# Another order of the seven Strassen products in an FFN up-projection, and a lower priority for the end of a norm

## Chip, cores and metric

The kernel runs on one core of one Trainium2 chip. The metric is the device time of one execution in microseconds (us), given as the median of the runs; lower is better.

## What is computed

One layer of a transformer with two half-step FFNs (macaron form) around a token mixer, on 1024 tokens of width 1024, d_ff 2816, all in fp32:

```python
def swiglu(h, w1, w3, w2):
    return (jax.nn.silu(h @ w1) * (h @ w3)) @ w2

def reference(x, ...):
    h = rmsnorm(x, ffn1_norm[l])
    x = x + 0.5 * swiglu(h, ffn1_w1[l], ffn1_w3[l], ffn1_w2[l])
    h = rmsnorm(x, mix_norm[l])
    x = x + token_mix(h, ...)          # differential attention and sparse attention
    h = rmsnorm(x, ffn2_norm[l])
    x = x + 0.5 * swiglu(h, ffn2_w1[l], ffn2_w3[l], ffn2_w2[l])
    return rmsnorm(x, final_norm)
```

The change lies in h @ w1 and h @ w3 of both FFNs and in the RMS norm behind FFN1.

## The kernel before

**Tiling.** Activations lie transposed, 128 features on the partitions and 512 tokens (TB) in a row; the 1024 tokens are two such halves, tb 0 and 1. Every fp32 product is made of three matmuls: operands are split into a high part (whi, hi) and a low rest (wlo, lo), and high x high, high x low and low x high are added up in PSUM. A weight is split by ScalarE (line 86, the high part) and VectorE (line 82, the low part: source minus high part). A matmul's stationary operand is 128 x 128 of a weight, its moving one 128 x 512 of the activations.

**FFN up-projection (ffn_up).** The 22 blocks f of 128 columns of w1 and w3 are taken in 11 pairs fp. The first two pairs (NPLAIN) are plain products. The other nine, per FFN, use the Winograd form of Strassen's algorithm on 2 x 2 blocks: the two f of a pair by the two halves of the 1024 features, against the two feature halves by the two token halves. It has seven products in place of eight. Each product has two results m (0 for w1, 1 for w3), and each m takes 4 blocks x 3 = 12 matmuls, so a product is 24 and a pair 168. The moving operands (B11, B21, B22 and T[0] to T[3]) are made once per FFN (right_sums). The weights are, by their names in the code: A11, A12 and A22 as loaded, and the sums S1 = A21 + A22, S3 = A11 - A21, S2 = S1 - A11, S4 = A12 - S2 (lines 352 to 355, on GpSimd, for the first pair on VectorE). S3 is written over a21 and S2 over a11, so a11 must be split before S2 is formed.

The products accumulate in three pairs of PSUM banks, X, Y and Z, each with m = 0 and 1, one buffer each:

| bank | products in their order | what reads the bank, and where |
|---|---|---|
| X | A11 B11, then A12 B21 on top | after A11: ScalarE copies it to s1 (line 343); after A12: Silu on ScalarE (348) and a multiply on VectorE (349) give c11 |
| Y | S2 T1, then S3 T2, then A22 T3 on top | after each: VectorE adds s1 into u2, u3 and c21 (363) |
| Z | S1 T0, then S4 B22 on top | after each: VectorE adds into u3 and u2 (370) |

A bank that is read in the middle of its sum must have been read before the next matmul accumulates into it. finish_a applies the Silu and the multiply (408, on GpSimd) and stores the result; act_sums forms four differences of a pair's results on GpSimd (378) and stores them in DRAM (379; saT in the trace), for the down-projection's own Strassen form. These run in place on u2, c21 and u3, whose tiles have one buffer. s1 has one buffer too.

**Weights around it.** a11 and a12 are loaded into two buffers (wst), a21, a22, s1 and s4 into one each, all by SP's DMA queue (line 332). Split weights have four slots (two pools of two). Between the products 13 jobs per FFN are handed out: left_sums loads two blocks of w2, forms four sums on VectorE (400) and stores them (402); plain_sums does the activations' differences for the two plain pairs, with four loads (386) into four tiles of their own.

**The end of FFN1 (ffn_down, after1).** The last of the seven down products updates x for the first half of the features of tb 1. For each block, after1 stores x, splits it for the next stage and adds its square to nacc (line 152). After the eighth, norm_final makes a matmul with a matrix of ones (tot, line 163) to sum over partitions, and the reciprocal root R from it (165, and 117 to 122), at a high priority (HOT = 400). The mixer's first products (gm, lines 49 to 51 under raw_unit) use the split x without R; their results are multiplied by R after the product. They have four banks.

**What sets the order.** The program is written with tiles and without semaphores. A planner at build time simulates the program and gives each engine a fixed queue: among the instructions whose inputs and buffers it takes to be ready it picks the one first in program order, shifted by a priority. At run time the queues run in order and wait for one another where data demand it. So TensorE's order need not be the program's, and the planner may cut a product in pieces.

Of the kernel before, what the change touches and what calls it, by code (L numbers as in the profile page):

```python
# [15 lines left out]
P = 128  # L16
T = 1024
# [137 lines left out]
        norm_final(K, tb)  # L155


def norm_final(K, tb):
    nc = K.nc
    del K.seen[tb]  # L160
    with K.tc.high_priority(offset=HOT):
        tot = K.pt.tile([P, TB], F32, tag="acc", name="tot")
        nc.tensor.matmul(tot, lhsT=K.ones, rhs=K.acc[tb], start=True, stop=True)  # L163
        m = K.np.tile([P, TB], F32, tag=f"nsq{tb * K.sq2}", name="nm")
        nc.vector.tensor_scalar(out=m, in0=tot, scalar1=1.0 / D, scalar2=EPS, op0=ALU.mult, op1=ALU.add)
        K.R[tb] = K.rp.tile([P, TB], F32, tag=f"R{tb}", name="R")
        K.rdone = newton_rsqrt(nc, K.R[tb], K.acc[tb], m, nc.vector)
# [97 lines left out]
def ffn_up(K, w13, w2, ctxt, ctx0, gi, first):  # L265
# [7 lines left out]
    def form(src):  # L273
        hi, lo = split_fresh(K, K.nw, src)
        K.nw += 1
        return hi, lo
# [34 lines left out]
    with ctx:  # L311
        rw = open_pool(K, ctx, "up_raw", 1)
        po = open_pool(K, ctx, "up_post", 1)
        ex = open_pool(K, ctx, "up_ex", 1)
        jobs = [lambda j=j: left_sums(K, ex, w2, j) for j in range(NF // 2)]
        jobs[4:4] = [lambda p=p: plain_sums(K, ex, p) for p in range(NPLAIN)]
        raw = lambda n: rw.tile([P, KD, P], F32, tag=n, name=n)
        B11, B21, B22 = K.h[0][0:h], K.h[0][h:], K.h[1][h:]

        def prod(o, w, m, x, start):  # L320
            for k in range(h):
                for i, (a, b) in enumerate(((0, 0), (0, 1), (1, 0))):
                    K.mark = nc.tensor.matmul(o, lhsT=w[a][:, m * h + k], rhs=x[k][b], start=start and k == 0 and i == 0,  # L323
                                              stop=k == h - 1 and i == 2, skip_group_check=True)

        for fp in range(NPLAIN, NF // 2):
            f0, f1 = 2 * fp, 2 * fp + 1
            a11 = K.wst.tile([P, KD, P], F32, tag="wst", name="a11")
            a12 = K.wst.tile([P, KD, P], F32, tag="wst", name="a12")
            a21, a22, s1, s4 = raw("a21"), raw("a22"), raw("s1"), raw("s4")  # L330
            for t, f, j in ((a11, f0, 0), (a21, f1, 0), (a22, f1, 1), (a12, f0, 1)):
                nc.sync.dma_start(out=t, in_=w13[f, j])
            u = {}
            for n in ("s1", "u2", "u3", "c21", "c11"):
                for m in range(2):
                    if n != "c11" or m == 0:
                        u[n, m] = po.tile([P, TB], F32, tag=f"{n}{m}", name=n)
            X, Y, Z = [[bank(n, m) for m in range(2)] for n in "XYZ"]

            w = form(a11)  # L340
            for m in range(2):
                prod(X[m], w, m, B11, True)
                nc.scalar.activation(out=u["s1", m], in_=X[m], func=AF.Copy)
            w = form(a12)
            for m in range(2):
                prod(X[m], w, m, B21, False)
            c = u["c11", 0]
            nc.scalar.activation(out=c, in_=X[0], func=AF.Silu)
            nc.vector.tensor_tensor(out=c, in0=X[1], in1=c, op=ALU.mult)
            store(f0, 0, c)  # L350
            se = nc.vector if fp == NPLAIN else nc.gpsimd
            se.tensor_tensor(out=s1, in0=a21, in1=a22, op=ALU.add)
            se.tensor_tensor(out=a21, in0=a11, in1=a21, op=ALU.subtract)
            se.tensor_tensor(out=a11, in0=s1, in1=a11, op=ALU.subtract)
            se.tensor_tensor(out=s4, in0=a12, in1=a11, op=ALU.subtract)
            done = (fp - NPLAIN) * len(jobs) // (NF // 2 - NPLAIN), (fp + 1 - NPLAIN) * len(jobs) // (NF // 2 - NPLAIN)
            for job in jobs[done[0]:done[1]]:
                job()
            for src, x, n in ((a11, T[1], "u2"), (a21, T[2], "u3"), (a22, T[3], "c21")):
                w = form(src)  # L360
                for m in range(2):
                    prod(Y[m], w, m, x, n == "u2")
                    nc.vector.tensor_tensor(out=u[n, m], in0=Y[m], in1=u["s1", m], op=ALU.add)  # L363
                if n == "c21":
                    finish_a(K, u[n, 0], u[n, 1], f1, 0, store)
            for src, x, n, f in ((s1, T[0], "u3", f1), (s4, B22, "u2", f0)):
                w = form(src)
                for m in range(2):
                    prod(Z[m], w, m, x, n == "u3")
                    nc.vector.tensor_tensor(out=u[n, m], in0=Z[m], in1=u[n, m], op=ALU.add)  # L370
                finish_a(K, u[n, 0], u[n, 1], f, 1, store if n == "u3" else lambda *_: None)
            act_sums(K, u["c11", 0], u["u2", 0], u["c21", 0], u["u3", 0], u["c21", 1], u["u2", 1], u["u3", 1], fp)


def act_sums(K, b11, b12, b21, b22, t1, t2, t4, j):
# [5 lines left out]

def plain_sums(K, ex, j):
    t = {}
    for n in ("B11", "B12", "B21", "B22"):
        t[n] = ex.tile([P, TB], F32, tag=n, name="pa")
        K.nc.sync.dma_start(out=t[n], in_=K.s_a[n][j])
    act_sums(K, t["B11"], t["B12"], t["B21"], t["B22"], t["B11"], t["B22"], t["B21"], j)


# [930 lines left out]
def body(tc, A, out):  # L1320
# [5 lines left out]
    with ExitStack() as ctx:  # L1326
# [27 lines left out]
        with ExitStack() as c0, ExitStack() as c1:  # L1354
            K.wpools = [K.whl, open_pool(K, c0, "whl2", B_W, side="right")]
            xp = open_pool(K, c1, "x", 1)
            K.np, K.sq2 = open_pool(K, c1, "norm1", 2), 1
            K.pt = open_pool(K, c1, "tot1", 2, True)
            K.x = x_tiles(xp, "x")
            log_exp(K)  # L1360
            first = []
            for tb in range(NTB):
                for k in range(KD):
                    if tb == 0 and k % 2 == 0:
                        first.append(load_fresh(K, k // 2, A["f1w13"][k // 4, k // 2 % 2]))
                    nc.sync.dma_start(out=K.x[tb][k], in_=A["x"][tb, :, k])
                    if tb == 0:
                        norm_split(K, 0, k, 0)
                    norm_stat(K, tb, k, nc.gpsimd if tb and k in (1, 3, 5) else nc.vector)
            K.sq2 = 0  # L1370

            def after1(tb, d):
                nc.sync.dma_start(out=K.s_x[tb][d], in_=K.x[tb][d])
                norm_split(K, tb, d, 1)
                norm_stat(K, tb, d, nc.vector, tb == 0)
            ffn(K, A["f1w13"], A["f1w2"], c1, 0, first, lambda tb, k: A["x"][tb, :, k], after1)
        mix(K)
        with ExitStack() as c2:
# [120 lines left out]
```

## Time and profile before

| | us |
|---|---|
| median of 3 runs | 3003.48 (2998.64 to 3005.93) |
| profiled execution, its own time | 3003.5 |
| its span, first to last instruction | 3001.7 |
| TensorE busy | 2872.7 (96%) |
| VectorE, ScalarE, GpSimd busy | 1956.4, 1274.2, 979.9 |
| FFN1: the nine Strassen pairs of the up-projection | 100.9 to 465.1 |
| FFN2: the same | 2409.0 to 2771.9 |

Engines are named as the profile does: PE is TensorE's matmul, PEld its weight load, DVE VectorE, ACT ScalarE, POOL GpSimd, SP the engine whose queue issues the DMAs (SPq). L323 is line 323. "Y<-tf,whi" is an instruction that writes tile Y from tiles tf and whi. PEclk is the granted TensorE clock as a share of 2.4 GHz. Time in brackets before an instruction is idle time of its engine, with what ended it. Times of a timeline are from the start of the span.

### The profile page before, as it was taken

The numbers are of one execution on the slowest core, as the hardware profiler recorded it, in microseconds if no ns is written. First come the engines' busy times: TensorE is split into PE (matmuls) and PEld (weight loads), VectorE is DVE, ScalarE is ACT, GpSimd is POOL, SyncE is SP. The second block draws the span as 40 slices with busy tenths as digits, with TensorE's granted clock in tenths as the row PEclk, the third lists the DMA queues.
The fourth block names the chain that finished last, engine by engine and source line by source line (L and its number), as shares of the span: only waits on it lengthen the run. The fifth ranks groups of instructions, "written<-read, shape, count | busy, mean of one in ns | idle before, by whom it ended". The sixth has DMA issues, their size and how long they took to land. (4 is left out here: it accounts for less than half of the span.)

```text
span 3001.7 us, 39937 instructions
## 1 busy us (share of the span) xinstructions
PE 2872.7 (96%) x14238; PEld 2395.9 (80%) x14238; DVE 1956.4 (65%) x3140; ACT 1274.2 (42%) x2195; POOL 979.9 (33%) x765
## 2 busy tenths in 40 slices
PE   9999999999999999799899999999999999999998
PEld 7777777887888778678788888888877877777886
DVE  8665666665687567676677777776433866566656
ACT  6322224442333245345566666666433422222443
POOL 4555551000044223222232333333232456553101
PEclk9999999999999999899999999999999999999999
DMA  4443448655456544544332234222842155445854
GB/s 140 173 162 133 174 163 303 200 191 150 148 184 241 192 159 148 185 160 164 130 109 85 85 115 160 77 83 73 301 141 100 62 204 171 141 164 181 288 183 147
DMA packets 212710, 478.19 MB, mean 159 GB/s; under 512 B 20896, under 2 KB 39584, under 8 KB 212512
## 3 DMA queue, kind: packets, MB, share of 16 engines
q1 hardware_dynamic: 212512, 475.65, 46.1%
q8 instruction: 112, 1.84, 0.3%
q14 instruction: 86, 0.70, 0.1%
HBM read 313.56 MB, written 162.00 MB: 158 GB/s over the span
## 5 line engine op out<-in xcount | busy, mean ns | idle before, releaser
L49 PE MATMUL gm<-hi,whi 128*128 128x512 f32 x880 | 353.4, 402 | 5.5 <-ACT whi L86 1.8
L51 PE MATMUL gm<-hi,wlo 128*128 128x512 f32 x880 | 350.2, 399 | 0.0
L50 PE MATMUL gm<-lo,whi 128*128 128x512 f32 x880 | 350.0, 398 | 0.0
L747 PE MATMUL S<-kt,qt 128*128 128x320 f32 (+5 forms) x1152 | 274.6, 352 | 45.7 <-ACT Pt L756 16.1
L82 DVE TENSOR_TENSOR tl<-tr,th 128x512 fp32r<-128x512 f32 (+2 forms) x384 | 236.3, 619 | 82.2 <-ACT th L86 78.5
L86 ACT ACTIVATE th<-tr 128x512 fp32r<-128x512 f32 (+2 forms) x384 | 204.1, 543 | 201.5 <-PE tr L797 197.2
L323 PE MATMUL Y<-tf,whi 128*128 128x512 f32 x864 | 275.0, 397 | 9.8 <-DVE u L363 9.8
L82 DVE TENSOR_TENSOR wlo<-st,whi 128x1024 fp32r<-128x1024 f32 x154 | 198.2, 1304 | 119.6 <-ACT whi L86 119.0
L754 DVE CUSTOM_DVE_ANT_0 S<-S,slab 128x896 f32<-128x896 f32 (+7 forms) x320 | 224.6, 709 | 71.5 <-PE S L747 67.1
L49 PE MATMUL acc<-whi 128*128 128x512 f32 (+1 forms) x628 | 243.4, 388 | 3.3 <-DVE u L370 3.3
L50 PE MATMUL acc<-wlo,whi 128*128 128x512 f32 (+1 forms) x628 | 243.4, 388 | 0.0
L51 PE MATMUL acc<-whi,wlo 128*128 128x512 f32 (+1 forms) x628 | 243.1, 389 | 0.0
L86 ACT ACTIVATE whi<-st 128x1024 fp32r<-128x1024 f32 x154 | 160.5, 1057 | 186.9 <-PE acc L51 124.6
L904 POOL TENSOR_SCALAR Ps<-Ps,l 128x384 f32<-128x384 f32 (+7 forms) x128 | 101.3, 791 | 421.8 <-DVE l L902 201.6
L747 PEld LDWEIGHTS S<-kt,qt 128*128 128x128 f32 x1152 | 183.6, 190 | 69.1 <-ACT Pt L756 17.2
L82 DVE TENSOR_TENSOR wlo<-a,whi 128x1024 fp32r<-128x1024 f32 x90 | 159.8, 1779 | 83.1 <-ACT whi L86 79.8
L323 PEld LDWEIGHTS Y<-tf,whi 128*128 128x128 f32 x864 | 162.6, 189 | 51.4 <-DVE u L363 14.7
L49 PEld LDWEIGHTS gm<-hi,whi 128*128 128x128 f32 x880 | 169.5, 193 | 39.9 <-issue 4.1
L51 PEld LDWEIGHTS gm<-hi,wlo 128*128 128x128 f32 x880 | 169.2, 192 | 36.8 <-DVE wlo L82 0.6
L50 PEld LDWEIGHTS gm<-lo,whi 128*128 128x128 f32 x880 | 169.2, 192 | 31.3
L323 PE MATMUL Y<-tf,wlo 128*128 128x512 f32 x432 | 171.0, 397 | 2.8 <-DVE wlo L82 2.8
L950 PE MATMUL o<-th,vt 128*128 128x256 f32 (+1 forms) x608 | 164.5, 287 | 1.8 <-ACT th L86 1.7
(313 smaller groups left out, 6968.6 us busy)
## 6 DMA issues: line engine op xcount, KB each, us to landing
wst<-in_win_dram SPq DMA_DIRECT2D x55, 512.0 KB
sw<-w2s SPq DMA_DIRECT2D x44, 512.0 KB
st<-sw SPq DMA_DIRECT2D x88, 256.0 KB
st<-saT SPq DMA_DIRECT2D x88, 256.0 KB
a<-in_f1w_dram SPq DMA_DIRECT2D x36, 512.0 KB
a<-in_f2w_dram SPq DMA_DIRECT2D x36, 512.0 KB
st<-saB SPq DMA_DIRECT2D x66, 256.0 KB
qt<-sq SPq DMA_DIRECT2D x128, 128.0 KB
```

What stands on the lines that cost most here:

```text
L49: first = nc.tensor.matmul(out, lhsT=w[0][:, wk], rhs=x[0], start=start, stop=False, skip_group_check=skip)
L50: nc.tensor.matmul(out, lhsT=w[0][:, wk], rhs=x[1], start=False, stop=False, skip_group_check=skip)
L51: nc.tensor.matmul(out, lhsT=w[1][:, wk], rhs=x[0], start=False, stop=stop, skip_group_check=skip)
L82: return nc.vector.tensor_tensor(out=lo, in0=src, in1=hi.bitcast(F32), op=ALU.subtract)
L86: nc.scalar.activation(out=hi, in_=src, func=AF.Copy)
L323: K.mark = nc.tensor.matmul(o, lhsT=w[a][:, m * h + k], rhs=x[k][b], start=start and k == 0 and i == 0, stop=k == h - 1 and i == 2, skip_g ...
L747: K.last = nc.tensor.matmul(S[:, o:o + n], lhsT=q, rhs=k[:, k0 + c:k0 + c + n], start=i == 0, stop=i == 1)
L754: nc.vector.tensor_tensor_reduce(out=sv, in0=sv, in1=mv, scale=-0.125, scalar=BIG, op0=ALU.add, op1=ALU.min, accum_out=nm)
L904: nc.gpsimd.tensor_scalar(out=p[:, 0:n], in0=p[:, 0:n], scalar1=l[:, c:c + 1], scalar2=1.0, op0=ALU.mult, op1=ALU.mult)
L950: nc.tensor.matmul(dst, lhsT=v, rhs=hi[:, b * P:(b + n) * P], start=False, stop=False, skip_group_check=True)
```

## The change

In ffn_up the order in the program becomes, per pair: S2 into Y, S1 into Z, A12 into X, S3 into Y, then the loads of the next pair and its A11 into X, then A22 into Y and S4 into Z. The A11 product of the first pair stands ahead of the loop. The tile s1 (now s0 and s1 of a new pool) gets two buffers. The adds of one product stand behind both of its m, apart from those of S4. The first weight splits of a pair are asked for in the order S2, S1, A12, S3, and A22 and S4 after the next A11. The jobs stay behind the A12 product. plain_sums takes its four tiles out of the two buffers that left_sums uses.

For FFN1's second token half the end of the norm (norm_final) is called by after1 with a priority of -60, so it stands behind instructions that follow it by about that many places, and not 400 places ahead.

```diff
-def norm_final(K, tb):
+def norm_final(K, tb, hot=HOT):
...
-    with K.tc.high_priority(offset=HOT):
+    with K.tc.high_priority(offset=hot):
...
+        po2 = open_pool(K, ctx, "up_s1", 2)
...
+        def load(fp):
...
+            r = [a11, a12] + [raw(n) for n in ("a21", "a22", "s1", "s4")]
+            for t, f, j in ((a11, f0, 0), (r[2], f1, 0), (r[3], f1, 1), (a12, f0, 1)):
                 nc.sync.dma_start(out=t, in_=w13[f, j])
+            return r
+
+        def first_product(r):
+            X = [bank("X", m) for m in range(2)]
+            w = form(r[0])
+            s = []
+            for m in range(2):
+                prod(X[m], w, m, B11, True)
+                s.append(po2.tile([P, TB], F32, tag=f"s{m}", name="s1"))
+                nc.scalar.activation(out=s[m], in_=X[m], func=AF.Copy)
+            return X, s
+
+        n0, n1 = NPLAIN, NF // 2
+        r = load(n0)
+        X, sv = first_product(r)
+        for fp in range(n0, n1):
...
+            se.tensor_tensor(out=s1, in0=a21, in1=a22, op=ALU.add)
+            se.tensor_tensor(out=a21, in0=a11, in1=a21, op=ALU.subtract)
+            se.tensor_tensor(out=a11, in0=s1, in1=a11, op=ALU.subtract)
+            se.tensor_tensor(out=s4, in0=a12, in1=a11, op=ALU.subtract)
+            ws2, ws1, wa12, ws3 = form(a11), form(s1), form(a12), form(a21)
+
+            def add(n, o, i):
+                for m in range(2):
+                    nc.vector.tensor_tensor(out=u[n, m], in0=o[m], in1=i[m], op=ALU.add)
             for m in range(2):
-                prod(X[m], w, m, B11, True)
-                nc.scalar.activation(out=u["s1", m], in_=X[m], func=AF.Copy)
-            w = form(a12)
+                prod(Y[m], ws2, m, T[1], True)
+            add("u2", Y, sv)
             for m in range(2):
-                prod(X[m], w, m, B21, False)
+                prod(Z[m], ws1, m, T[0], True)
+            for m in range(2):
+                prod(X[m], wa12, m, B21, False)
...
+            for m in range(2):
+                prod(Y[m], ws3, m, T[2], False)
+            add("u3", Y, sv)
+            for m in range(2):
+                nc.vector.tensor_tensor(out=u["u3", m], in0=Z[m], in1=u["u3", m], op=ALU.add)
+            finish_a(K, u["u3", 0], u["u3", 1], f1, 1, store)
+            if fp + 1 < n1:
+                r = load(fp + 1)
+                X, nxt = first_product(r)
+            wa22, ws4 = form(a22), form(s4)
+            for m in range(2):
+                prod(Y[m], wa22, m, T[3], False)
+            add("c21", Y, sv)
+            finish_a(K, u["c21", 0], u["c21", 1], f1, 0, store)
+            for m in range(2):
+                prod(Z[m], ws4, m, B22, False)
+                nc.vector.tensor_tensor(out=u["u2", m], in0=Z[m], in1=u["u2", m], op=ALU.add)
+            finish_a(K, u["u2", 0], u["u2", 1], f0, 1, lambda *_: None)
             act_sums(K, u["c11", 0], u["u2", 0], u["c21", 0], u["u3", 0], u["c21", 1], u["u2", 1], u["u3", 1], fp)
+            sv = nxt
...
-    for n in ("B11", "B12", "B21", "B22"):
-        t[n] = ex.tile([P, TB], F32, tag=n, name="pa")
-        K.nc.sync.dma_start(out=t[n], in_=K.s_a[n][j])
+    for i in range(2):
+        w = ex.tile([P, 2, TB], F32, tag=f"w{i}", name="pa")
+        for z, n in enumerate((("B11", "B12"), ("B21", "B22"))[i]):
+            t[n] = w[:, z]
+            K.nc.sync.dma_start(out=t[n], in_=K.s_a[n][j])
...
-                norm_stat(K, tb, d, nc.vector, tb == 0)
+                norm_stat(K, tb, d, nc.vector, True)
+                if tb and len(K.seen) and K.seen[1] == KD:
+                    norm_final(K, 1, -60)
```

## Rows read from the trace of the kernel before

**Rows 1.** The page's first lines: busy us (share of the span), instructions.
```profile
span 3001.7 us, 39937 instructions
PE 2872.7 (96%) x14238; PEld 2395.9 (80%) x14238; DVE 1956.4 (65%) x3140; ACT 1274.2 (42%) x2195; POOL 979.9 (33%) x765
```

**Rows 2.** Waits of weight loads, FFN1's stage: us in total, times, longest.
```profile
PEld Y L323 <- DVE u L363: 7.0, 6, 2.4
PEld Z L323 <- DVE u L370: 3.7, 2, 1.8
PEld Y L323 <- DVE wlo L82: 2.4, 1, 2.4
PEld Z L323 <- DVE wlo L82: 1.1, 2, 0.6
```

**Rows 3.** The same view, FFN2's stage; its L370 row reads as in rows 2.
```profile
PEld Y L323 <- DVE u L363: 7.7, 6, 2.4
...
PEld Z L323 <- DVE wlo L82: 3.3, 2, 2.2
PEld Y L323 <- DVE wlo L82: 1.3, 1, 1.3
```

**Rows 4.** Busy us per engine (instructions), PEclk, DMA share, GB/s: both stages.
```profile
100.90:465.10 364.20, 354.55 (x1514) 285.23 (x1514) 223.81 (x209) 96.29 (x117) 200.58 (x98) 0.99 0.49 171
2409.00:2771.90 362.90, 351.59 (x1513) 282.91 (x1513) 223.17 (x209) 96.75 (x117) 201.07 (x98) 1.00 0.49 172
```

**Rows 5.** The same view (PE, PEld, DVE, ACT, POOL), short stretches behind stalls.
```profile
412.00:416.00 4.00, 4.00 (x12) 3.12 (x11) 2.55 (x4) 1.58 (x2) 0.22 (x1) 0.57 0.58 236
416.00:420.00 4.00, 4.00 (x19) 3.19 (x18) 1.90 (x3) 1.69 (x2) 3.92 (x2) 1.00 0.00 0
690.00:692.00 2.00, 2.00 (x6) 1.59 (x5) 0.82 (x2) 0.36 (x1) 0.00 (x0) 0.50 1.02 411
```

**Rows 6.** Timeline of VectorE and the weight loads: start, us, instruction.
```profile
365.15 2.88 DVE L400 TENSOR_TENSOR w2s<-w2s 128x512 f32<-128x512 f32 x1
368.68 0.30 PEld L323 LDWEIGHTS Y<-tf,whi 128*128 128x128 f32 x2 [0.82 <-DVE u L363]
```

**Rows 7.** Timeline: next pair's first load, T stores issued, u2's add.
```profile
383.52 0.19 PEld L323 LDWEIGHTS X<-hi,whi 128*128 128x128 f32 x1
391.68 3.93 SPq L379 DMA_DIRECT2D saT<-u  x3
395.51 0.69 DVE L363 TENSOR_TENSOR u<-Y,s 128x512 f32<-128x512 f32 x1 [2.78 <-DMA saT<-u]
```

**Rows 8.** Timeline of VectorE and the weight loads at FFN1's end.
```profile
683.03 1.22 DVE L82 TENSOR_TENSOR wlo<-wst,whi 128x1024 fp32r<-128x1024 f32 x1
684.83 0.68 DVE L152 TENSOR_TENSOR nacc<-nacc,nsq 128x512 f32<-128x512 f32 x1
685.57 0.50 PEld L163 LDWEIGHTS tot<-nacc,ones 128*128 128x128 f32 x2 [4.87 <-DVE nacc L152]
688.49 0.29 PEld L49 LDWEIGHTS gm<-hi,whi 128*128 128x128 f32 x1 [2.42 <-issue]
```

**Rows 9.** Timeline: GpSimd's sums of a next pair, and S2's split.
```profile
333.42 2.43 POOL L354 TENSOR_TENSOR a<-s,a 128x1024 f32<-128x1024 f32 x1 [5.41 <-DVE wlo L82]
335.88 1.06 ACT L86 ACTIVATE whi<-a 128x1024 fp32r<-128x1024 f32 x1 [1.29 <-POOL a L354]
336.97 2.43 DVE L82 TENSOR_TENSOR wlo<-a,whi 128x1024 fp32r<-128x1024 f32 x1 [1.64 <-ACT whi L86]
361.38 2.78 POOL L352 TENSOR_TENSOR s<-a,a 128x1024 f32<-128x1024 f32 x1 [9.13 <-DVE wlo L82]
364.23 3.25 POOL L353 TENSOR_TENSOR a<-a,a 128x1024 f32<-128x1024 f32 x1
```

More of the change, by code (lines that the diff above doesn't have):

```diff
@@ L324, in prod @@
                                               stop=k == h - 1 and i == 2, skip_group_check=True)
-        for fp in range(NPLAIN, NF // 2):
+        def load(fp):
             f0, f1 = 2 * fp, 2 * fp + 1
@@ L329, in ffn_up @@
             a12 = K.wst.tile([P, KD, P], F32, tag="wst", name="a12")
-            a21, a22, s1, s4 = raw("a21"), raw("a22"), raw("s1"), raw("s4")
-            for t, f, j in ((a11, f0, 0), (a21, f1, 0), (a22, f1, 1), (a12, f0, 1)):
+            r = [a11, a12] + [raw(n) for n in ("a21", "a22", "s1", "s4")]
+            for t, f, j in ((a11, f0, 0), (r[2], f1, 0), (r[3], f1, 1), (a12, f0, 1)):
                 nc.sync.dma_start(out=t, in_=w13[f, j])
+            return r
[12 more added lines that the diff above has]
+        for fp in range(n0, n1):
+            f0, f1 = 2 * fp, 2 * fp + 1
+            a11, a12, a21, a22, s1, s4 = r
             u = {}
-            for n in ("s1", "u2", "u3", "c21", "c11"):
+            for n in ("u2", "u3", "c21", "c11"):
                 for m in range(2):
@@ L337, in ffn_up @@
                         u[n, m] = po.tile([P, TB], F32, tag=f"{n}{m}", name=n)
-            X, Y, Z = [[bank(n, m) for m in range(2)] for n in "XYZ"]
-            w = form(a11)
+            Y, Z = [[bank(n, m) for m in range(2)] for n in "YZ"]
+            se = nc.vector if fp == n0 else nc.gpsimd
+            se.tensor_tensor(out=s1, in0=a21, in1=a22, op=ALU.add)
[6 more added lines that the diff above has]
+                    nc.vector.tensor_tensor(out=u[n, m], in0=o[m], in1=i[m], op=ALU.add)
             for m in range(2):
-                prod(X[m], w, m, B11, True)
-                nc.scalar.activation(out=u["s1", m], in_=X[m], func=AF.Copy)
-            w = form(a12)
+                prod(Y[m], ws2, m, T[1], True)
+            add("u2", Y, sv)
             for m in range(2):
-                prod(X[m], w, m, B21, False)
+                prod(Z[m], ws1, m, T[0], True)
+            for m in range(2):
+                prod(X[m], wa12, m, B21, False)
             c = u["c11", 0]
@@ L350, in ffn_up @@
             store(f0, 0, c)
[L351 to L356, printed above, removed]
+            done = (fp - n0) * len(jobs) // (n1 - n0), (fp + 1 - n0) * len(jobs) // (n1 - n0)
@@ L357, in ffn_up @@
             for job in jobs[done[0]:done[1]]:
                 job()
[L359 to L371, printed above, removed]
+            for m in range(2):
+                prod(Y[m], ws3, m, T[2], False)
```

## The prediction

> **What bounds the kernel now.** I began with the page's totals [rows 1]: TensorE is busy for 2872.7 of 3001.7 us, 96%. On one core with one engine that full, an edit that leaves the number of matmuls alone can only win back TensorE's gaps, about 129 us in all by this count, and only those that lie in the code it touches. So I next looked at what TensorE waits for. A gap of the matmul row is hidden in part by the modelled end of the matmul before it, so I read the waits of the weight loads (PEld), which start once per matmul and show the gap itself, in each of the two up-projection stages [rows 2, 3]. The reader is to see two kinds. In FFN1 the Y and Z products wait 7.0 and 3.7 us for the adds at lines 363 and 370; in FFN2 7.7 and 3.7 us (the row of line 370 is the same in both). Those are bank turns: an add has to read a PSUM bank before the next product may accumulate into it. The second kind, 2.4 + 1.1 us and 1.3 + 3.3 us, is the low half of a weight (wlo, line 82) that is not ready.
>
> How much of the stage this is: the stages last 364.2 and 362.9 us [rows 4]. FFN2's, less its 16.0 us of waits, is 346.9 us for its 1512 matmuls (9 pairs x 7 products x 24), 0.2294 us each, so a product of 24 takes 5.5 us and a pair 38.5 us. FFN1's, less its 14.2 us, is 350.0 us, 3.1 us more, and that is clock: after the wait that ends near 412 the granted clock is 0.57 and TensorE starts 12 matmuls in 4 us, against 19 in the 4 us after [rows 5], so 7 x 0.229 = 1.6 us went there, and the other 1.5 us near the first pair. At 0.50 to 0.57 this is mostly the 1.2 GHz level, against 2.4 GHz elsewhere. FFN2 had waits as long and its clock stayed at 1.00 [rows 3, 4].
>
> VectorE (224 us), ScalarE (96 us) and GpSimd (201 us) have room in a stage of 364 us [rows 4]; none of them is the bound. They matter because their queues run in order. The wait of 0.82 us at 368.68 [rows 6] shows it: line 400's sum took 2.88 us to 368.03, and the add that frees the bank came only behind it.
>
> **The order of the products.** Nothing is added or removed on TensorE, and per pair the same adds, copies, splits, sums and stores remain. What moves is the distance between a product and the next into the same bank. Before, S2, S3 and A22 go into Y one after another, so between the two there is only the other half (m) of the same product, 12 matmuls or 2.75 us, unless the planner slips in something else. After, the order is S2 (Y), S1 (Z), A12 (X), S3 (Y), the next pair's A11 (X), A22 (Y), S4 (Z), the next S2 (Y). Each Y bank now rests for 5.5 to 11 us, X for 5.5, Z for more. The longest delay of a bank turn in the rows is 2.4 us beyond the 2.75 [rows 2, 3], so 5.5 us covers all of them. Gain: 7.0 + 3.7 + 7.7 + 3.7 = 22.1 us in 16 waits; of each some 0.04 us is the normal space between loads, so 21.5 us. With them goes the low clock at 412, 1.6 us, since a wait for line 363 came right before it. Ends: none of it (the planner puts the products back side by side), to all 16 waits and the clock, 23.1 us.
>
> The Trainium skill, "TensorE: Matmul & The Clock Gate", section "A second HAM failure mode: psum-queue depth-cycling", has it that short idles between groups of matmuls that cycle through PSUM banks make the clock fall again and again. If every one of the 16 waits cost the 1.6 us seen once, 26 us more would come back. The trace doesn't agree: FFN2's stage has eight such waits and a mean clock of 1.00, so this is left out of the sum.
>
> *Last pair of a stage.* There is no next A11, so A22 follows S3 in Y directly and the old turn remains, once per FFN. Its rows go from about nothing to 2.4 us; I take 1 us each, 2 us lost, near the 0.82 of a plain turn [rows 6].
>
> *First pair.* S2's operand is summed on VectorE just before it is needed, A11 runs first in both orders, and A12 may fill in. The waits for wlo in both stages, 8.1 us, I leave as they are: value 0, ends +8 (they vanish, with the clock at the first pair 9.6) and -8 (A12's split comes after S2's and S1's in the new order and they double).
>
> *Loads and splits of the next pair.* Their four loads on SP's queue, the split of A11 and its product move 11 us ahead against A22 and S4. A11's buffer is free once S2 is split and S4 summed; that is 20 us before the new place, so nothing waits there. The load of the next A22 has to wait until this pair's A22 is split, and stands on SP's queue ahead of A12's load and of stores; A12 is needed 60 us later, the stores by nobody near. Its chain is the third rival.
>
> *The second S2 add.* The tile of u2 is single. Its add for the next pair must wait until this pair's T3 and T2 are stored. Before, that came 12.0 us after S4's end (383.52 to 395.51, released by the store issued from 391.68) [rows 7]. After, S2 follows S4, so VectorE wants to add 5.5 us after S4's end and waits about 6.5 us, the second half about 2 us more. Who waits: S3, which is 16.5 us after S4's end, so it has 2 to 4 us of cover. If that cover is gone, each pair loses the excess. Price here 0.
>
> *plain_sums* now shares the buffers of left_sums: two jobs queue behind one another's stores, and nobody on TensorE waits for them. 0. The second s1 buffer only allows the early A11 product; 0.
>
> **The norm at FFN1's end.** The last sum into nacc ends at 684.83 + 0.68 = 685.51; tot's weight load starts at 685.57 after a gap of 4.87 us, so TensorE's work before it had its last load until 680.70; the first gm load starts only at 688.49 [rows 8]. The gm matmuls that are first need their low weight half, ready at 683.03 + 1.22 = 684.25 [rows 8]. So with tot behind them gm can start 688.49 - 684.25 = 4.2 us earlier; tot then costs its own 1.2 us (an estimate: the gap of 2.42 before gm's load is tot's run at the low clock, and half of it is its run at the high one); and the clock, 0.50 with 6 matmuls in 2 us from 690 [rows 5], against 9 at the other level, gives back 3 x 0.229 = 0.7 us per 2 us, 1.5 us over some 4 us, if the shorter idle doesn't drop it. 4.2 - 1.2 + 1.5 = 4.5 us. Ends: +8 (the whole of 680.70 to 688.49) to -4 (the reciprocal root for the second half, R, comes as much later as gm comes sooner, and its readers hold the gm banks). Who waits for R: the scaling of the second half's results, a whole product (5.5 us) behind the first; four gm banks stand between, so I take 4.5.
>
> **Sum.** 21.5 + 1.6 - 2 + 0 + 4.5 = 25.6 us. The profiled execution took 3003.5 us, of which 3001.7 is the span; the median of the runs is 3003.48, so no correction. Predicted 3003.5 - 25.6 = 2978 us. With the ends +9.6 for wlo and +3.5 for the norm it is 2965; the mixing stage between is planned anew from another start and may give or take some 3 us, so 2962 at the low end.
>
> **Rivals.**
> *The order doesn't hold.* The planner, not the program, sets TensorE's order. It may again lay Y beside Y, as it did before by cutting A12 into pieces. Then only the norm's 4.5 us come: 2999. For it: it did so already. Against it: in the new program order the product next in line is always ready, so there is nothing to swap for. Chance 0.12.
>
> *Half of it turns into other waits.* u2's add holds VectorE's queue for up to 6.5 us per pair, behind which weight splits stand; the rows show such a hold already, 2.78 us at 395.51 [rows 7]. If 8 pairs per FFN each lose 0.7 us, 11 us are given back: 2989. For it: the hold grows in each pair. Against it: each split has its slot free 16.5 us before its product. Chance 0.18.
>
> *Slower: the sums of the next pair come too late.* Place: the loop from S1's end (which frees the weight slot of A22) over A22's split, A22's load, three sums on GpSimd and S2's split to the next S2. Counted from the start of S2: S1 ends at 11; split 1.06 + 2.43 to 14.5; load 3.8 for 256 KB [rows 7], so 5 taken for 512 KB, 19.5; sums 2.78 + 3.25 + 2.43 to 28; split 3.5 to 31.5 [rows 9]; needed at 38.5. Slack 7 us, less when a multiply of the same queue comes between. It decides from the point where the chain is late by more than 25.6 / 16 = 1.6 us per pair, 8.6 us above my count. At 4 us per pair: 16 x 4 = 64 lost, 3042. The Trainium skill, "SBUF — State Buffer", section "Who interferes with whom", says that a GpSimd sum and a VectorE operation with two SBUF inputs lock each other out for whole instructions, which would stretch this chain; by rows 6 line 400 does take 2.88 us, and the sums above are already measured beside VectorE. Chance 0.08.
>
> **How the numbers follow.** Forecast as worked out (2962 to 2985): 0.62; half of it: 0.18; order not held: 0.12; slower: 0.08. A measurement here can tell about 0.3%, 9 us, from no change, so faster means below 2994.5: 0.62 + 0.15 of the second = 0.77. Within 0.3%: 0.12 + 0.03 = 0.15. Slower 0.08. To leave out no more than 2 in 10 the range runs from 2962 over the half case to 2996.
>
> **What would show it.** Right: in the changed profile the waits for the adds of Y and Z shrink below 3 us per stage, the stages last about 350 us, no low clock near 412, and gm begins before tot. Wrong: Y still in runs next to Y; waits of S2 products for wlo in every pair, with GpSimd's sums at their back; VectorE waiting for the store of T2 or T3 with weight splits behind; or R late and gm waiting for it.

## The result, and the profile after

The changed kernel takes 2983.85 us (median of 4 runs, 2981.74 to 2987.14) against 3001.09 us for the kernel before on the same chip: ratio 0.995, 95% interval 0.9935 to 0.9965. That is 17.2 us or 0.5% less, more than the 0.3% that a measurement here can tell. The forecast was 2978 us with a range of 2962 to 2996: the sign and the range held, the saving came to two thirds of the 25.6 us forecast. The profiled execution took 2981.74 us, so between the two profiled executions lie 21.8 us.

The page's head, to be read against [rows 1]:

```profile
span 2979.9 us, 39953 instructions
...
PE 2862.8 (96%) x14238; PEld 2392.2 (80%) x14238; DVE 1981.2 (66%) x3140; ACT 1269.7 (43%) x2195; POOL 969.4 (33%) x765
```

TensorE runs the same 14238 matmuls; only its gaps shrank. VectorE has the same 3140 instructions and is busy 25 us longer, which the last section returns to. Busy time by stretch for the two stages, columns as in [rows 4]:

```profile
101.60:454.40 352.80, 350.51 (x1513) 284.74 (x1512) 235.69 (x208) 96.64 (x119) 194.85 (x97) 1.00 0.50 176
2399.20:2751.20 352.00, 349.40 (x1514) 283.44 (x1513) 236.75 (x211) 98.03 (x121) 194.99 (x98) 1.00 0.51 178
```

The stages went from 364.2 and 362.9 to 352.8 and 352.0 us: 11.4 + 10.9 = 22.3 us, as much as lies between the two profiles. From FFN1's last weight load of the down-projection (acc) to FFN2's first Strassen product it was 1728.5 us before and is 1728.3 now; nothing was won outside the two stages. The waits of weight loads in FFN1's stage (all that is left on line 324, the products' line, now) and in FFN2's, against [rows 2, 3]:

```profile
PEld Y L324 <- issue: 3.1, 2, 2.2
```

```profile
PEld Y L324 <- issue: 3.0, 2, 1.9
PEld Y L324 <- DVE u L367: 1.1, 2, 0.8
```

Four rows per stage with 14 to 16 us became one or two with 3 to 4. The waits for low weight halves (wlo) are gone, and most of those for the adds. TensorE's order, read from its weight loads, is now in whole products of 24: Y X Y Z, Y Z X, and again, as the program has it; only the first and the last pair are cut.

From this order one can count the matmuls between a product and the next into the same bank. Before, 19 to 29 stood between two products of a pair in a Y bank, and not the 12 that the prediction took: in every pair the planner had put pieces of A12 and S1 there. Now 36 or 60 stand there, apart from the first and the last pair. The waits of Y for its adds before were all at A22, behind S3. One such turn before (with the lines of [rows 6] beside these) and one in the changed kernel:

```profile
361.78 0.19 PEld L323 LDWEIGHTS Y<-tf,wlo 128*128 128x128 f32 x1
362.42 2.82 DVE L82 TENSOR_TENSOR wlo<-s,whi 128x1024 fp32r<-128x1024 f32 x1
367.95 0.68 DVE L363 TENSOR_TENSOR u<-Y,s 128x512 f32<-128x512 f32 x1
```

```profile
401.67 0.19 PEld L324 LDWEIGHTS Y<-tf,wlo 128*128 128x128 f32 x1
402.73 3.41 DVE L82 TENSOR_TENSOR wlo<-s,whi 128x1024 fp32r<-128x1024 f32 x1
406.06 2.89 DVE L431 TENSOR_TENSOR w2s<-w2s 128x512 f32<-128x512 f32 x1
408.87 0.68 DVE L367 TENSOR_TENSOR u<-Y,s 128x512 f32<-128x512 f32 x1
410.10 0.42 PEld L324 LDWEIGHTS Y<-tf,whi 128*128 128x128 f32 x2
```

In both the first half of S3 has its last load (361.78, 401.67), a split and a sum of w2 stand in VectorE's queue, and the add ends only 6.9 and 7.9 us after that load. Before, A22's turn came after 26 matmuls, 6.1 us, and waited 0.82 us; now it comes after 36, 8.4 us, and doesn't wait. Over both stages the adds behind S3 end 4.2 us after its last load on the mean before (10.6 at most) and 5.7 us now (9.4 at most). So the adds have not become earlier; the turns come later. In the 14 profiles of this document all 124 waits of Y for its adds, those that the rows call "issue" among them, end 0.05 to 0.12 us after the add does.

What is left, FFN1's two waits, in the timeline of TensorE's loads, VectorE, ScalarE, GpSimd and SP's transfers; of every timeline only the rows that the reading needs are shown. First the smaller:

```profile
239.94 0.69 DVE L367 TENSOR_TENSOR u<-Y,s 128x512 f32<-128x512 f32 x1 [8.38 <-DMA saT<-u]
240.75 0.30 PEld L324 LDWEIGHTS Y<-tf,whi 128*128 128x128 f32 x2 [0.85 <-issue]
```

This is u2's single tile: S2's add stood 8.38 us for the store of the pair before, and S3's product, next into the bank, started 0.85 us late. Then the larger:

```profile
252.25 1.28 POOL L407 TENSOR_TENSOR pa<-pa 128x512 f32<-128x512 f32 x1 [1.22 <-DMA pa<-saB]
253.49 2.40 POOL L360 TENSOR_TENSOR a<-a,a 128x1024 f32<-128x1024 f32 x1
255.84 1.29 POOL L407 TENSOR_TENSOR pa<-pa 128x512 f32<-128x512 f32 x1
257.09 2.39 POOL L361 TENSOR_TENSOR a<-s,a 128x1024 f32<-128x1024 f32 x1
259.51 1.06 ACT L86 ACTIVATE whi<-a 128x1024 fp32r<-128x1024 f32 x1 [9.66 <-POOL a L361]
260.61 1.23 DVE L82 TENSOR_TENSOR wlo<-a,whi 128x1024 fp32r<-128x1024 f32 x1 [12.34 <-ACT whi L86]
261.75 2.31 DVE L82 TENSOR_TENSOR wlo<-s,whi 128x1024 fp32r<-128x1024 f32 x1
263.99 1.28 DVE L367 TENSOR_TENSOR c<-Y,s 128x512 f32<-128x512 f32 x2
264.78 0.30 PEld L324 LDWEIGHTS Y<-tf,whi 128*128 128x128 f32 x2 [2.23 <-issue]
```

Read it from below. S2's product waits 2.23 us at 264.78 for the bank that the adds into c21 (263.99) must read first. These stood in VectorE's queue behind two weight splits, the first of which waited 12.34 us for ScalarE's half, that one 9.66 us for GpSimd's sum of line 361, and between GpSimd's sums stand two of plain_sums (line 407). A22's product into that bank had its last load before 257.15. The row says "issue", so the profile names no releaser; the cause is read from the times, since the first of the two adds ends 0.12 us before the load. In FFN2 the same two places wait 1.05 and 1.94 us.

The clock behind the larger wait, PE, PEld, DVE, ACT, POOL, PEclk:

```profile
264.00:268.00 4.00, 3.19 (x10) 2.62 (x11) 2.95 (x4) 1.58 (x2) 3.54 (x2) 0.76 0.25 59
268.00:272.00 4.00, 4.00 (x16) 3.17 (x16) 2.95 (x4) 1.60 (x3) 1.96 (x2) 0.81 0.87 315
```

One stretch below full clock follows the 2.23 us wait: that product of 24 takes 6.96 us and not 5.5, so 1.5 us. The Trainium skill, "TensorE: Matmul & The Clock Gate", section "A second HAM failure mode: psum-queue depth-cycling", tells of a kernel that cycles through PSUM banks and in which TensorE's short idles between groups of matmuls come often enough to make the clock swing between its two levels. Here no such swing shows: the clock dips once in FFN1 behind two waits, and FFN2's mean is 1.00 with four.

The end of FFN1, against [rows 8]:

```profile
675.97 0.50 PEld L163 LDWEIGHTS tot<-nacc,ones 128*128 128x128 f32 x2 [4.88 <-DVE nacc L152]
678.89 0.29 PEld L49 LDWEIGHTS gm<-hi,whi 128*128 128x128 f32 x1 [2.42 <-issue]
```

These are the same two gaps, 4.88 and 2.42 us, in the same order. The lower priority did not move tot.

### The profile page after: what moved, and what is told of

Read it like the earlier page. It is cut to its first block, busy times and chain, and to the rows that moved or that the text cites. A ratio compares the mean times of both kernels' runs of the same rounds, so it can differ in the third digit from the quotient of the medians.

```text
span 2979.9 us, 39953 instructions
## 1 busy us (share of the span) xinstructions
PE 2862.8 (96%) x14238; PEld 2392.2 (80%) x14238; DVE 1981.2 (66%) x3140; ACT 1269.7 (43%) x2195; POOL 969.4 (33%) x765
## 4 chain that ended last, share of the span: by engine, by line
PE 75%; DMA 9%; DVE 6%; issue 3%; ACT 3%; POOL 2%; SPq 1%; DVEq 0%; ACTq 0%; POOLq 0%
PE Y L324 7%; PE gm L49 6%; PE gm L51 6%; PE gm L50 6%; PE S L778 6%; PE X L324 5%; PE Z L324 5%; PE acc L49 5%; PE acc L51 5%; PE acc L50 5%; PE tr L828 4%; PE o L982 2%; PE o L981 2%; DMA sg<-smx 1%; DMA kt<-sk 1%
## 5 line engine op out<-in xcount | busy, mean ns | idle before, releaser
L82 DVE TENSOR_TENSOR wlo<-a,whi 128x1024 fp32r<-128x1024 f32 x90 | 136.4, 1518 | 107.4 <-ACT whi L86 107.4
```

Of the source, the lines that this page charges most:

```text
L82: return nc.vector.tensor_tensor(out=lo, in0=src, in1=hi.bitcast(F32), op=ALU.subtract)
```

## The experiments

All times in us; the ratio is to the kernel before on the same chip, with its 95% interval.

| kernel | median | ratio |
|---|---|---|
| changed kernel, beside the prediction | 2983.85 | 0.9950 (0.9935 to 0.9965) |
| e1 its norm as before | 2979.0 | 0.9930 (0.9916 to 0.9943) |
| e2 its plain_sums first | 2983.5 | 0.9941 (0.9928 to 0.9953) |
| e3 its A11 late again | 2981.48 | 0.9938 (0.9919 to 0.9956) |
| e4 its norm behind the first gm product | 2978.35 | 0.9923 (0.9909 to 0.9936) |
| e5 kernel before, Y adds made twice | 3029.72 | 1.0102 (1.0079 to 1.0125) |
| e6 changed kernel, Y adds made twice | 2989.09 | 0.9966 (0.9953 to 0.9979) |
| e7 early A11, but S2, S3, A22 in a row | 2994.72 | 0.9981 (0.9969 to 0.9994) |
| e8 changed kernel again | 2981.83 | 0.9936 (0.9917 to 0.9955) |
| e9 kernel before, norm behind the first gm product | 2993.47 | 0.9987 (0.9972 to 1.0002) |
| e10 as e4, again | 2977.32 | 0.9934 (0.9916 to 0.9953) |
| e11 as e4, A11 late | 2973.99 | 0.9915 (0.9897 to 0.9932) |
| e12 changed kernel again, beside e10 and e11 | 2987.21 | 0.9956 (0.9940 to 0.9971) |

The 13 runs of the changed kernel reach from 2978.3 to 2989.0 (median 2982.7), the 46 of the kernel before from 2992.8 to 3008.1 (median 2999.6). One run, and one profile with it, stands up to 9 us from its median, so rows below 5 us are read by whether they come again at the same place, not by the total.

**The theory** was that the order inside a pair gives each bank the time that its add needs. **The rivals**: that the early A11 product, which lets the next pair's work start sooner, is what counts; that the norm carries a part; that the residual waits come from plain_sums.

**e1: the norm's end as before.**

```diff
-                norm_stat(K, tb, d, nc.vector, True)
-                if tb and len(K.seen) and K.seen[1] == KD:
-                    norm_final(K, 1, -60)
+                norm_stat(K, tb, d, nc.vector, tb == 0)
```

> The changed kernel with the norm's end as before (HOT, called from norm_stat); the new order of the products stays. Theory: the lower priority moved nothing, since the queues of all five engines hold the same instructions in the same order with it and without it, so this takes the same time as the changed kernel, 2984 us within 3 us, and tot is again waited for about 4.9 us with gm behind it. Rival: the priority was worth part of the 4.5 us forecast, then 2987 to 2989 us.

It took 2979.0, no longer than the changed kernel. The instruction order on all five engines is the same with and without this part, so it is worth nothing as it stands; the trace has the waits of 4.87 and 2.42 us at tot and gm again. That two equal programs gave 0.9930 and 0.9950 is the scatter named above.

**e3: the next pair's A11 last in its pair, as before; the order inside the pair as changed.**

```diff
-            if fp + 1 < n1:
-                r = load(fp + 1)
-                X, nxt = first_product(r)
             wa22, ws4 = form(a22), form(s4)
...
-            sv = nxt
+            if fp + 1 < n1:
+                r = load(fp + 1)
+                X, sv = first_product(r)
```

> The new order without the early A11: loads and A11 product of the next pair stand behind S4 and the act_sums, so A22 follows S3 in Y again in the program. Theory: what counts is the distance between two products in one bank; the planner finds other work for part of it (it lays S1 and pieces of A12 between), so most of the gain stays and a few turns of 0.7 us come back, 2985 to 2991 us. Rival: the gain is the lead that the early A11 gives to the weights' splits and sums; then it is lost, 2996 us or more, with waits for wlo.

2981.5, and stages of 352.3 and 349.8 us from first to last load: the whole gain is there, and my own expectation of 2985 to 2991 was too dear. But the early A11 isn't gone. In TensorE's order 14 of its 24 matmuls (11 in one pair) stand ahead of A22 all the same; the planner took them forward. ScalarE's copy of A11's first half, at 211.79 for one, comes while A22 still runs. So 23 or 26 matmuls stand between S3 and A22 in a bank, not 12 (but for the last pair). That is no more than in the kernel before, but here the adds behind S3 end at most 7.1 us after its last load (10.6 before), and 0.8 us of waits is left at this turn. The run shows that A11 need not stand there whole; what comes with none of it there no run shows. FFN1's waits are 3.2 us for low weight halves at X and 1.9 us for the adds at Y.

**e5 and e6: every add of s1 to a Y bank made twice** (the second writes the same again, 0.68 us more each), in the kernel before and in the changed one.

```diff
-                    nc.vector.tensor_tensor(out=u[n, m], in0=o[m], in1=i[m], op=ALU.add)
+                    for _ in range(2):
+                        nc.vector.tensor_tensor(out=u[n, m], in0=o[m], in1=i[m], op=ALU.add)
```

> The kernel before with every add that reads a Y bank made twice on VectorE: 0.68 us more per add, 6 adds per pair, 108 in both stages (73 us more work for VectorE, which is 62 % busy there). If what the order buys is the distance between two products into one bank, the kernel before has no distance to spare: its Y products follow one another at 12 to 24 matmuls (2.75 to 5.5 us), so it loses 10 to 30 us against 3000, 3010 to 3030, with the waits of Y loads for the add at twice to four times their 14.7 us. The rival, that the gain comes from the early A11 and not from the banks' distance, expects about as much loss here as in the changed kernel with the same edit (difference under 5 us).

> The changed kernel with the same doubled adds. Distance: each Y bank rests for 24 matmuls (5.5 us) or more, an add twice as long (1.36 us) still fits, so at most 5 us are lost against 2979 to 2984: 2979 to 2989; the gap to the kernel before with the same edit grows from 17 to 22 us to 25 to 45 us. The rival: the loss is that of the kernel before, and the gap stays at 17 to 22 us.

The kernel before lost 30.6 us by the medians, the changed one 7.3 (2989.09 against 2981.83 for the changed kernel on that chip); the distance between the two grew from 17.3 to 40.6. The theory expects that and the rival does not. Waits of weight loads in FFN1's stage of e5, then in FFN2's stage of e6 (its worse one):

```profile
PEld Y L323 <- DVE u L364: 13.0, 9, 2.9
PEld Z L323 <- DVE wlo L82: 6.8, 3, 5.6
PEld Y L323 <- DVE wlo L82: 2.2, 1, 2.2
```

```profile
PEld Y L324 <- DVE u L368: 5.5, 4, 2.5
PEld Y L324 <- issue: 3.3, 4, 1.5
```

In e5 the waits of Y for its adds rose from 7.0 + 7.7 to 13.0 + 13.2 us, 1.8 times (I had said at least twice). But e5 is not the old order with longer adds alone: the planner laid it anew, with 36 matmuls between S2 and S3 in half of the turns, and the waits of Z for its adds nearly went (0.4 us after 7.4). By the profiles the two stages are 20.8 us longer, of which 14.9 are waits: 4.6 for adds of both banks, 10.3 for splits that came late in the fuller queue. The rest goes with the clock, 0.98 in the two stages against 0.99 and 1.00. The changed kernel with doubled adds kept its order up to the last pair. An add of twice the length fits there but for a few turns; 7.3 us is over the 5 us that I gave it.

**e7: the early A11 kept, S2, S3 and A22 written one behind the other into Y, then S1, A12, next A11, S4.**

```diff
-            ws2, ws1, wa12, ws3 = form(a11), form(s1), form(a12), form(a21)
+            ws2 = form(a11)
...
             add("u2", Y, sv)
-            for m in range(2):
-                prod(Z[m], ws1, m, T[0], True)
...
+            ws3 = form(a21)
+            for m in range(2):
+                prod(Y[m], ws3, m, T[2], False)
+            add("u3", Y, sv)
+            wa22 = form(a22)
+            for m in range(2):
+                prod(Y[m], wa22, m, T[3], False)
+            add("c21", Y, sv)
```

> The changed kernel with its early A11 product kept, but S2, S3 and A22 written one behind the other again (all into Y), then S1, A12, the next A11, S4. TensorE's instruction order has 17 or 18 matmuls from one product of a Y bank to the next (3.9 to 4.1 us) instead of 24 and more. If the distance is what counts, most of the gain goes: stages of 357 to 364 us and 2992 to 3003 in all. If the early A11 is what counts, it stays at 2979 to 2986 with stages of 352 to 353 us.

2994.7, stages of 360.2 and 359.4 us from first to last load: the number came as the distance theory says, but not for its reason. FFN1's waits, and the cause of the two at X:

```profile
PEld X L324 <- DVE wlo L82: 5.0, 2, 2.5
PEld Z L324 <- ACT whi L86: 3.0, 1, 3.0
PEld Y L324 <- DVE u L367: 0.9, 1, 0.9
```

```profile
234.55 5.21 DVE L434 TENSOR_TENSOR w2s<-w2s 128x512 f32<-128x512 f32 x3 [2.25 <-DMA w2s<-in_f1w_dram]
239.69 3.40 DVE L82 TENSOR_TENSOR wlo<-a,whi 128x1024 fp32r<-128x1024 f32 x1
243.14 0.19 PEld L324 LDWEIGHTS X<-hi,wlo 128*128 128x128 f32 x1 [2.51 <-DVE wlo L82]
```

The 17 or 18 matmuls that I had expected were a miscount: 23 stand between S3 and A22 in a bank, and over 40 between S2 and S3, but for 12 in the first pair. So at S3 and A22 e7's turns are as close as in the kernel before, which waited 14.7 us there, and e7 doesn't wait at all: its adds behind S3 end at most 2.6 us after the last load. The bank waits left are 0.9 and 0.4 us per stage. No count of matmuls is enough or too few by itself; a turn waits when the add ends after it. What e7 lost is the readiness of weights: A12's low half comes behind three sums of w2 and has its product at once behind it, four times 2.51 us in both stages, and the first pair waits 3.0 us twice. Without any of its waits its stages take 350.4 and 350.9 us, against 349.5 and 347.7 in the changed kernel, which goes with its lower clock (0.99 against 1.00). So an order in a pair has two things to serve, the banks and the splits, and the changed order serves both.

**e2: plain_sums' jobs ahead of left_sums' (`jobs[4:4]` becomes `jobs[0:0]`).**

> The changed kernel with the two plain_sums jobs handed out first (first and second Strassen pair) and not as fifth and sixth. Theory: the four waits left in the two stages (0.85 and 2.23 us in FFN1, 1.05 and 1.94 us in FFN2, with 1.5 us of low clock behind the second) come from plain_sums: its eight GpSimd sums, loaded through the shared buffers, stand in GpSimd's queue between the sums that S2 of the fifth pair needs. Then the waits go, and 6 to 9 us with them: 2975 to 2978 us. Rival: they come from the single tile of u2, which waits for the stores of T3 and T2 in every pair; then they stay, 2984 us.

2983.5, no gain. The waits near 240 and 264 went, so they hang on the place of plain_sums. Others came, 2.63 us the longest:

```profile
323.50 2.89 DVE L431 TENSOR_TENSOR w2s<-w2s 128x512 f32<-128x512 f32 x1
326.32 3.42 DVE L82 TENSOR_TENSOR wlo<-s,whi 128x1024 fp32r<-128x1024 f32 x1
329.66 2.86 DVE L431 TENSOR_TENSOR w2s<-w2s 128x512 f32<-128x512 f32 x1
332.44 0.68 DVE L367 TENSOR_TENSOR u<-Y,s 128x512 f32<-128x512 f32 x1
333.17 0.30 PEld L324 LDWEIGHTS Y<-tf,whi 128*128 128x128 f32 x2 [2.63 <-DVE u L367]
```

```profile
323.46 2.39 POOL L359 TENSOR_TENSOR s<-a,a 128x1024 f32<-128x1024 f32 x1 [7.57 <-DMA a<-in_f1w_dram]
325.93 2.73 POOL L360 TENSOR_TENSOR a<-a,a 128x1024 f32<-128x1024 f32 x1
328.74 3.24 POOL L361 TENSOR_TENSOR a<-s,a 128x1024 f32<-128x1024 f32 x1
```

Here left_sums' sums of w2 (0.69 us at 322.29 in the same run, without GpSimd beside it) take 2.9 us each while GpSimd's sums run, and the add stands behind them. So moving plain_sums only moved the waits: other work in the queues made an add late by as much elsewhere. That fits the Trainium skill, "SBUF — State Buffer", section "Who interferes with whom": a VectorE operation with two SBUF inputs contends with a GpSimd instruction that reads SBUF.

**e8 and e12: the changed kernel unedited.**

> The changed kernel once more, unedited, beside these: how far two profiles of one program differ. 2979 to 2987; stages of 351 to 354 us; the waits for the adds of Y under 3.5 us per stage, at the same places of the program if they belong to the order of the queues, elsewhere if they come from the moment. The wait of tot for nacc, 4.9 us, again at the same place.

> The changed kernel, unedited, as the comparison for the three runs beside it: 2979 to 2984.

2981.8 and 2987.2 (expected up to 2984: a miss of 3 us by the second). The waits near 240 and 264 of FFN1 and their twins in FFN2 came again in e8 (0.86, 1.12, 0.48, 1.50 us); they belong to the order of the queues. So did 4.87 us at tot in e12.

**e4, e9 to e11: the norm's end behind the first gm product.** norm_final is called in the mixer after the 24 matmuls of the first gm product, and tot takes a gm bank, so that it stands there in program order. Then the step that the change meant is really made. The scaling of cR and sR by R is cut into two halves for it, and nacc and the norm's small tiles take tiles of R and of the mixer. e9 has this on the kernel before, e11 with the A11 of e3.

```diff
-        tot = K.pt.tile([P, TB], F32, tag="acc", name="tot")
+        tot = (K.gm if K.late and tb else K.pt).tile([P, TB], F32, tag="gm" if K.late and tb else "acc", name="tot")
...
-        for kv in range(2):
-            drain([raw_unit(K, kv)])
+        u = raw_unit(K, 0)
+        for _ in range(KD):
+            next(u)
+        norm_final(K, 1, 0)
+        K.late = False
+        scale_cs(K, 1)
+        drain([u, raw_unit(K, 1)])
```

> The changed kernel with the end of FFN1's norm for tb 1 moved in the program to behind the first gm product of the mixer, tot in a gm bank, nacc in the tile of R. Here tot does stand behind 24 gm matmuls in TensorE's queue. Theory: that was the step that failed; gm then starts when its low weight half is ready, 4 us earlier, and some 4.5 us are gained against the changed kernel: 2979 us. Rival: R comes later, the results of the second token half and the scaled cosine tables wait for it, and the gain is given back: 2983 to 2986 us.

> The kernel before with the norm's end placed behind the first gm product in program order, tot in a gm bank; the FFN order is that of the kernel before. If the 4.5 us of the norm were sized right and only the priority failed to move tot, this alone gives what it gave on the changed kernel (profiled 4.6 us from FFN1's last sum to FFN2's first product: 1723.7 against 1728.3): 2992 to 2997 against 2999, the wait of 4.87 us at tot and of 2.42 us at gm gone. The rival, that the gain of that run was scatter, expects 2998 to 3001 and the stretch at 1728.

> The changed kernel with the norm's end behind the first gm product, as in the earlier run, beside the unedited changed kernel on one chip: 2975 to 2980, 4 to 6 us below the changed kernel, if the 4.87 + 2.42 us at tot and gm are really on the path. If the two differ by under 2 us, the earlier difference was scatter between jobs.

> The same with the next pair's A11 product written last in its pair again, so that only the order within a pair and the norm's end differ from the kernel before. If the early A11 buys nothing, as its single run says (2981.5 against 2979 to 2984), 2974 to 2980, equal to the run beside it within 3 us. If it buys something that the norm's move hides, 2980 to 2986.

Weight loads of e4 from FFN1's last one on, and VectorE's write of vt:

```profile
670.96 0.19 PEld L51 LDWEIGHTS acc<-whi,wlo 128*128 128x128 f32 x1
671.19 0.19 PEld L49 LDWEIGHTS gm<-hi,whi 128*128 128x128 f32 x1
676.65 0.42 PEld L163 LDWEIGHTS tot<-R,ones 128*128 128x128 f32 x2
708.96 0.69 DVE L613 TENSOR_TENSOR vt<-gm,R 128x512 f32<-128x512 f32 x1 [1.11 <-DMA sraw<-vt]
709.76 0.71 PEld L616 LDWEIGHTS tr<-ident,vt 128*128 128x128 f32 x4 [4.37 <-issue]
```

gm follows acc without a gap, tot comes 5.5 us later and waits for nothing; 4.88 + 2.42 = 7.3 us of gaps are gone. A transpose (tr) then waits 4.37 us at 709.76, where the kernel before waits 0.26 us and the changed one not at all; the same in e9 to e11 (4.26, 4.25, 4.70). It reads vt, which has one buffer, and VectorE writes it at 708.96, when the store of the vt before (sraw) has landed. From FFN1's last load to FFN2's first product the four take 1723.7, 1724.1, 1723.3 and 1725.4 us; the ten profiles without the move take 1724.7 to 1730.1, nine of them above 1726. Beside e12, e10 is 9.9 us faster and e11 13.2; e9 is 6.0 below the kernel before, its interval just touching 1. So the step is worth some 4 to 5 us by the stretch when it is made, and part of what it frees is given back at tr. e11, at 2974.0, is the best of all and beats both kernels; against e10 (2977.3) the intervals overlap. So where the program writes A11 makes no difference that can be told here; in e11 too the planner has 14 of its matmuls ahead of A22.

## Why the prediction was right, and where its size was off

*What bounds the kernel.* Right: with the same matmuls the time moved by TensorE's gaps in the two stages and hardly anywhere else.

*The bank turns, 21.5 us.* Right in place and kind: the waits for the adds fell from 22.1 us (lines 363 and 370) to 7.2, of which 1.1 go by the add's name and 6.1 as "issue". What removed them is the later turn, as forecast: in the changed kernel the adds end no earlier, and adds of twice the length cost it less (e6) than the old order (e5). But the sizes behind the term were misread. I took 12 matmuls, 2.75 us, for the distance before; it was 24 to 28 at the turns that waited, 5.5 us and more, because the planner had already put other work there. I also counted only whole products for the distance after, 24 or 48, without the other half of the same product, so it is 36 or 60. By the rows, 2.4 us of wait beyond 6.1 asks for some 8.5 us, and the 5.5 us of my argument would not have covered it; the real 8.4 us nearly do. That the conclusion held is luck on this point. The early A11 is no rival to this but a part of it: it is the 24 matmuls that stand between S3 and A22. How few of them would do no run shows below the 11 to 14 of e3.

The stages gave 22.3 us between the two profiles, against 21.5 + 1.6 - 2 = 21.1 forecast. That agreement is in part luck, for two terms that I set at 0 were not 0 and nearly cancel. The wlo waits, 8.1 us, vanished (I had the end +9.6 in the range). For the 3.7 us at the first pair the reason is that the planner runs S1 there while S2's split is made; for the 4.4 us at Z in later pairs none was looked for. And 6.1 us of waits came at two places of each FFN where none had been: 3.1 in FFN1, as shown above, and 3.0 in FFN2; 1.1 us at A22 are left.

*The low clock at 412.* Gone, as forecast; a new one of 1.5 us came at 264. Net about nothing, for 1.6 forecast. Nor does the dip belong to that wait: e9 has the old order and a wait of 2.37 us at the same place, and its clock is 1.00 from 412 to 416, where the profile before has 0.57 [rows 5].

*Last pair, 2 us lost.* It ends in Y36 Z11 Y12 Z13 and shows no wait: the planner had S4's matmuls to put between.

*The second S2 add.* The hold is there, but mostly shorter than the 6.5 us of the working, 0.2 to 3.3 us; only once per FFN is it longer, 8.38 us at 239.94 and 8.59 in FFN2. The cover of 2 to 4 us held but for 0.85 and 1.05 us there, in the pair with plain_sums' work among the stores that it waits for.

*plain_sums, 0.* Wrong in kind: I looked at its buffers and not at GpSimd's queue, in which its adds stand between the sums of the next pair. That is the place of the third rival (sums, S2's split), and the chain came late there by 1.9 to 2.2 us once per stage. The rival with 4 us in every pair did not come.

*The norm, 4.5 us.* This is the step that failed. Its size was about right, as e4, e9 and e10 show when tot really stands behind gm; but I took it for granted that a lower priority puts it there. It changed no instruction's place on any engine. Why not stays open: tot's tile is asked for ahead of the gm tiles in the program, and the planner may give out PSUM in program order, but no run shows it, and e4 changed the place, the bank and the priority together. I had priced "the order doesn't hold" as a rival for the FFN and had none for the norm.

*The sum.* Of the 25.6 us, 4.5 were never there, which leaves 21.1; the two profiled executions differ by 21.8. The medians differ by 17, since the profile before was a slow sample: at 3003.5 it is 3.9 us above the median of the 46 runs. e9, with the same FFN order, waits 7.0 + 3.6 and 7.9 + 3.7 us for the same adds, but its stages take 360.2 and 360.9 us from first to last load, against 363.9 and 362.6 in the profile before; its clock in FFN1 is 1.00 against 0.99. Two profiles of the old order and three of the new (the changed kernel, e8, e12) give 362.1 - 352.3 = 9.8 and 361.8 - 352.3 = 9.5, 19.3 us in all. A base of 2999.6 and a gain of 17 to 19 would have been the better forecast of the time.

## What to carry to other kernels

When several products accumulate into one PSUM bank that is read in between, count the matmuls from a product to the next into the same bank in the order that the engine runs, not in the program's, and set that time against the end of the reader, which counts from its place in its queue and not from its own length. Then see that the weights' splits keep pace in the new order, since e7 lost nearly as much there (17 us of waits) as the banks had gained. A lower priority need not move an instruction: compare the two instruction orders before putting a price on it. And where terms are a few us, price them against several profiles of the same kernel, not against one.

## What I had not expected of the hardware

*VectorE gets longer beside GpSimd.* The changed kernel gives VectorE the same instructions in a stage and 235.7 us of work for 223.8; e3, with A11 written late, needs 218.0. The line of w2's sums in FFN1's stage, by form (count, busy, mean ns of one), in the changed kernel:

```profile
L431 DVE TENSOR_TENSOR w2s<-w2s 128x512 f32<-128x512 f32 x42 | 56.3, 1340 | 27.4 <-DMA w2s<-in_f1w_dram 25.1 <-DMA saB<-u 2.1
L82 DVE TENSOR_TENSOR wlo<-s,whi 128x1024 fp32r<-128x1024 f32 x18 | 46.1, 2560 | 1.7 <-ACT whi L86 1.7
```

and in the kernel before:

```profile
L400 DVE TENSOR_TENSOR w2s<-w2s 128x512 f32<-128x512 f32 x44 | 45.5, 1034 | 24.2 <-DMA w2s<-in_f1w_dram 24.1
L82 DVE TENSOR_TENSOR wlo<-s,whi 128x1024 fp32r<-128x1024 f32 x18 | 32.9, 1828 | 0.3 <-ACT whi L86 0.2
```

Of S1's and S4's splits (`wlo<-s`) in the stage, those with no GpSimd instruction beside them take 1.22 us each, 10 before and 4 now; those with one take 2.6 us on the mean before, 2.9 now. The other splits (`wlo<-a`) went the other way, from 1.83 to 1.52 us on the mean. VectorE has 117 us to spare in a stage, but not at every turn: the 3.41 us split at 402.73 and the sum behind it are what made that add end 7.9 us after S3's last load.

*One execution is not the kernel.* Runs of the kernel before beside e9 to e12 lie between 2992.8 and 3008.1, 15 us apart, and in a stage two profiles with nearly the same waits for the same adds (before and e9) differ by 2 to 4 us.
